# Streaming encoder layer on one core: weight-block sums fetched two units ahead, with other PSUM banks and another order of products

## The chip, the core and the metric

One core of a Trainium2 chip runs the whole program. The time is device microseconds from launch to the last output. The kernel before takes 1981.8 us (median of 3 runs, 1981.6 to 1982.52).

## What is computed

One inference step of a hybrid layer on 576 frames (512 of a prompt, 64 of a sample), model width 1024:

```python
h = h + 0.5 * swiglu(rmsnorm(h, g1), w_ffn1_in, w_ffn1_out)
h = h + mixer(rmsnorm(h, gm))
h = h + 0.5 * swiglu(rmsnorm(h, g2), w_ffn2_in, w_ffn2_out)
y = rmsnorm(h, final_norm)
def swiglu(x, w_in, w_out):
    a, b = split(x @ w_in, 2)            # w_in 1024 x 8192, w_out 4096 x 1024
    return (silu(a) * b) @ w_out
```

The mixer is one wide projection that feeds an SSD scan, a band attention and an mLSTM; their outputs are projected, gated, merged and projected once more. All is float32.

## The kernel before

**Products.** A float32 operand is split (`split`, L271) into a rounded part and a remainder: ScalarE (ACT) casts to `ph` (L272), VectorE (DVE) subtracts to `pl` (L273). A product of a 512 x 128 weight block with a 512 x 288 half of the activations is then 4 x 3 = 12 matmuls of 288 columns (`product`, L584, matmuls on L591). Most of the two feed-forward stages and of the mixer's projection is done in *units*: a 2 x 2 block product with seven products in place of eight. The weights of a unit are four blocks q0 to q3 in HBM; the operands on the weights' side are q0, q2, q3 (products A11, A22, A21) and the sums X1 = q0+q1, X2 = q1+q2, X3 = X1+q2, X4 = X3+q3. In each feed-forward stage a stream has 40 units, in the mixer 35.

**Fetching.** `fetch` (L436) loads q0,q1 into a tile `x12` of the ring `wx` (three buffers of 512 KB) from the SP queue (L444), then adds q1,q2 onto it with a second, accumulating transfer from GpSimd's (POOL's) queue (L445): that makes X1 and X2. POOL's queue waits in its turn until the load has landed. Three more loads from SP (L449) bring q0, q2, q3 into the ring `wr`. `operand` (L452) makes X3 and X4 by POOL additions (L455): in the feed-forward stages in place in `x12`, in the mixer in a ring `wy`.

**Order.** `stream` (L470) writes out the list of uses: round n holds the products of unit n marked 0 and those of unit n-1 marked 1 in `order`. In the feed-forward stages (L747) a round is X1, A22 of n-1, A11, A21 of n-1, X3, X4, X2 of n-1. Splits are written down AHEAD = 5 products before use (`make`, L477); `make` fetches unit n+1 when unit n's first operand, X1, is made. The third `wx` buffer is that of unit n-2, free when the X2 split of that unit is done, which is the split just before. Within these dependences and the priorities a planner (the framework's timeline scheduling) lays down the order in which each engine and queue gets its instructions; PE's order in the trace is not quite the written one. Every engine and queue works in order.

**Banks.** X1, X3, A22 and X2 of a unit add up in one PSUM bank, X4 and A21 in a second, A11 has a third (L749): two sets of three banks, alternating. Each partial sum is read out before the next product may add to it: `swiglu` (L594) copies X1 to `g` (ACT, L602) and X3 and X4 to `P` (ACT, L607), `residual` (L622) adds to `R` on DVE (L630). So product X3 waits for the copy L602, and X1 of unit n+2 for the last readout (L618 or L630) of unit n.

**Mixer.** `pairs` (L497) uses `stream` too, with its own order and banks, and the same `fetch`.

**Squares.** `sumsq` (L276) and the norms use tiles `sq` (two) and `na` (one) of 128 x 320 in the pool `small`.

Of the kernel before, what the change touches and what calls it, by code (L numbers as in the profile page):

```python
# [25 lines left out]
F32 = mybir.dt.float32  # L26
F32R = mybir.dt.float32r
AF = mybir.ActivationFunctionType
ALU = mybir.AluOpType
# [12 lines left out]
FBUFS = {"P": 5, "g": 5, "s": 3}  # L42
WBUFS = {"wr": 5, "wx": 3, "wy": 2, "ph": 6, "pl": 6}
PBUFS = {"s": 2, "x": 1, "v": 1}
# [34 lines left out]
class Hybrid:  # L79
    def __init__(self, ctx, tc, I, O):  # L80
        self.tc, self.nc, self.I, self.O = tc, tc.nc, I, O
        self.plan = []
        self.splan = []
# [57 lines left out]
    def hidden_tiles(self, name):  # L141

        self.hidden.close()
        self.hidden.enter_context(self.pools(name, yp=dict(side="right")))
        self.YH, self.YL = self.pair_of(self.yp, [128, 8, T], ("YH", "YL"))
# [34 lines left out]
    def ps(self, tag):  # L180
        return self.psp.tile([128, 512], F32, name="ps_" + tag, tag=tag, bufs=self.pbufs[tag])

    def sm(self):
# [92 lines left out]
    def sumsq(self, x, k, h, acc, first=None):  # L276
        nc = self.nc
        a, n = HALVES[h]
        if first is True or first is None and k == 0:
            nc.scalar.activation(acc[:, :n], x[:, k, a:a + n], AF.Square)  # L280
            return
        sq = self.small.tile([128, 320], F32, name="sq", tag="sq", bufs=2)
        nc.scalar.activation(sq[:, :n], x[:, k, a:a + n], AF.Square)
        nc.vector.tensor_tensor(acc[:, :n], acc[:, :n], sq[:, :n], op=ALU.add)
# [41 lines left out]
    def norm(self, x, g0, hi, lo):  # L326

        nc = self.nc
        with self.tc.high_priority(offset=1500):
            for h, (a, n) in enumerate(HALVES):  # L330
                sl = slice(a, a + n)
                acc = self.small.tile([128, 320], F32, name="na", tag="na", bufs=1)
                for k in range(8):
                    self.scaled(x, g0, hi, lo, k, sl)
                    self.sumsq(x, k, h, acc)
                pt = self.ps("x")
                self.total([acc], n, pt)
                nc.scalar.copy(self.rs[:, sl], self.spread(pt, n)[0][:, :n])

    def norm_first(self, x, g0, hi, lo, pin):  # L340
# [4 lines left out]
        for h, (a, n) in enumerate(HALVES):  # L345
            sl = slice(a, a + n)
            sq = self.sqp.tile([128, 8, n], F32, name="sq0", tag=f"sq{h}")
            pt = self.ps("x")
# [15 lines left out]
    def norm_out(self, x, g0, out):  # L364

        nc = self.nc
        with self.tc.high_priority(offset=1500):
            for h in (1, 0):
                a, n = HALVES[h]
                sl = slice(a, a + n)  # L370
                acc = self.small.tile([128, 320], F32, name="na", tag="na", bufs=1)
                pt = self.ps("x")
                for k in range(8):
                    if h == 0 and k == 7:
                        sq = self.small.tile([128, 320], F32, name="sq", tag="sq", bufs=2)
                        nc.scalar.activation(sq[:, :n], x[:, k, sl], AF.Square)
                        self.total([acc, sq], n, pt)
                    else:
                        self.sumsq(x, k, h, acc)
# [55 lines left out]

    def fetch(self, desc):  # L436

# [6 lines left out]
        nc.sync.dma_start(x12, src[:, 0:2, :])  # L444
        nc.gpsimd.dma_start(x12, src[:, 1:3, :], accum_op=ALU.add)  # L445
        raw = {"x12": x12}
        for q in (2, 3, 0) if self.mixer else (0, 2, 3):
            raw[q] = self.ring("wr")
            nc.sync.dma_start(raw[q], src[:, q, :])  # L449
        return raw  # L450

# [18 lines left out]
    def stream(self, seq, order, banks):  # L470
# [3 lines left out]
        uses = [(n - d, t) for n in range(len(seq) + 1) for d, t in order if 0 <= n - d < len(seq)]  # L474
        raw, ops, st = {}, {}, {}

        def make(n, t):  # L477
            for m in (n, n + 1):
                if m < len(seq) and m not in raw:
                    raw[m] = self.fetch(seq[m][0])  # L480
            ops[n, t] = self.operand(raw[n], t)
# [177 lines left out]
    def ffn(self, x, g0, win, wout, name, last=(0, 1)):  # L659
# [85 lines left out]
        for c in range(1, 4):  # L745
            seq += [unit(c, j) for j in range(2)] + [out(c - 1, m) for m in range(4)] + [unit(c, j) for j in range(2, 8)]
        order = ((0, self.T_X1), (1, self.T_A22), (0, self.T_A11), (1, self.T_A21), (0, self.T_X3), (0, self.T_X4),  # L747
                 (1, self.T_X2))
        self.stream(seq, order, lambda n: {t: 3 * (n % 2) + i for i, t in enumerate((self.T_X1, self.T_A11, self.T_X4))})  # L749
        self.drain()  # L750
# [608 lines left out]
    def run(self):  # L1359
        nc, tc = self.nc, self.tc  # L1360
        x = self.R1
        with self.ffn_phase("a"):
            xin = self.I["xT"].rearrange("(k p) t -> p k t", p=128)
            with self.pools("a0", sqp=None):
                self.setup()
# [34 lines left out]
    def branches(self, x):  # L1400
        nc = self.nc
        units = {"a": (self.attn_gemm, self.attn), "m": (self.ml_gemm, self.ml), "s": (self.ssd_gemm, self.ssd)}
        got = {u: units[u[0]][0](u[1]) for u in ORDER[:2]}
        with self.pools("m0", xp=None, op=None):
            self.XH, self.XL = self.pair_of(self.xp, [128, 8, T], ("XH", "XL"))
            self.norm(x, C_GM, self.XH, self.XL)
# [12 lines left out]
            self.plain([(("gate", 0), 1.0, put_gate)])  # L1419
        with self.pools("m", fp=None):  # L1420
            na = self.fp.tile([128, T], F32, name="sumsq")
            self.ss = [na[:, a:a + n] for a, n in HALVES]
# [113 lines left out]
```

## Time and profile before

| | |
|---|---|
| median of 3 runs | 1981.8 us |
| the profiled execution, its own time | 1983.52 us |
| its span, first to last instruction | 1981.8 us |
| PE (matmuls) busy | 1901.4 us, 96%, 13889 |
| DVE, ACT, POOL busy | 1461.5, 1083.3, 673.0 us |
| mean granted TensorE clock | 0.982 |
| mean DMA rate | 150 GB/s |
| chain that ended last | PE 35%, DMA 8%, DVE 3%, ACT 3%; by line L591 21%, the landing of `wx` 6% |
| first feed-forward stream (L591) | from 66 us |
| mixer | about 600 to 1215 us |
| second feed-forward stream (L591) | 1454 to 1913 us |

Busy shares are averages over these stages. A line such as "PE acc L591 <- ACT g L602: 4.2, 4, 1.8" says that matmuls of L591 began 4 times right after a wait that ACT's line 602 ended, 4.2 us in all, the longest 1.8 us. The ends of matmuls are modelled.

### The profile page before, as it was taken

The page shows a single profiled execution, that of the slowest core. Times are in us where ns is not written, and L with a number is a line of the kernel's source. Part 1 is how long each engine was busy: PE and PEld are TensorE (multiplying, and loading weights), DVE is VectorE, ACT ScalarE, POOL GpSimd, SP SyncE. Part 2 cuts the span into 40 slices and gives each one's busy share as a digit, 9 for nine tenths or more (in the row PEclk, how much of TensorE's full clock was granted, in tenths as well). Part 3 has the DMA queues.
Part 4 walks back from the last instruction along what each step waited for, and adds up shares of the span by engine and source line. Part 5 has one row for each costly group of instructions (what it writes and reads, how often), then busy time and mean ns, then how long its engine had stood idle before and what let it go on. Part 6 is the DMA issues. An engine that isn't in the chain of part 4 may idle for free.

```text
span 1981.8 us, 37575 instructions
## 1 busy us (share of the span) xinstructions
PE 1901.4 (96%) x13889; PEld 1824.5 (92%) x13889; DVE 1461.5 (74%) x2727; ACT 1083.3 (55%) x2487; POOL 673.0 (34%) x662
## 2 busy tenths in 40 slices
PE   9999999999999889999989998899999999999998
PEld 8899999999999759978889897899999999999998
DVE  8987877877668958667676774665798787787765
ACT  4554554544545577677586874333555454454444
POOL 5343333333202215322443443351233333333311
PEclk9999999999999879999999998999999999999999
DMA  7267666666742535753656668652236666656631
GB/s 215 72 158 174 151 155 163 149 167 168 184 128 96 131 104 145 212 149 110 178 150 180 162 169 246 203 167 86 75 97 160 160 150 161 162 151 161 174 109 63
DMA packets 130079, 297.04 MB, mean 150 GB/s; under 512 B 14416, under 2 KB 26320, under 8 KB 129896
## 3 DMA queue, kind: packets, MB, share of 16 engines
q1 hardware_dynamic: 100648, 208.03, 33.0%
q0 software_dynamic: 19760, 72.10, 19.9%
q10 hardware_dynamic: 9488, 14.52, 2.4%
q8 instruction: 109, 1.79, 0.4%
q14 instruction: 74, 0.61, 0.1%
HBM read 274.04 MB, written 20.56 MB: 149 GB/s over the span
## 4 chain that ended last, share of the span: by engine, by line
PE 35%; DMA 8%; DVE 3%; ACT 3%; issue 2%; POOL 1%; ACTq 0%; DVEq 0%; POOLq 0%; SPq 0%
PE acc L591 21%; PE acc L244 12%; DMA wx<-in_sblk 6%; DMA R<-scr_rows 1%; DVE pl L273 1%; ACT ph L272 1%; DMA y<-ys 1%; ACT R L1188 1%; DVE TL L273 0%; PE ps_s L1206 0%; PE ps_v L1228 0%; PE ps_x L1235 0%; DVE P L639 0%; DVE g L639 0%; DMA ys<-g 0%
## 5 line engine op out<-in xcount | busy, mean ns | idle before, releaser
L591 PE MATMUL acc<-TH,ph 128*128 128x288 f32 x3220 | 959.0, 300 | 31.9 <-ACT g L602 10.4
L591 PE MATMUL acc<-TL,ph 128*128 128x288 f32 x3220 | 952.8, 297 | 0.1
L591 PE MATMUL acc<-TH,pl 128*128 128x288 f32 x3220 | 944.1, 297 | 6.6 <-DVE pl L273 6.1
L591 PEld LDWEIGHTS acc<-TH,ph 128*128 128x128 f32 x3220 | 605.6, 189 | 52.3 <-ACT g L602 13.4
L591 PEld LDWEIGHTS acc<-TH,pl 128*128 128x128 f32 x3220 | 604.6, 189 | 14.3 <-DVE pl L273 11.1
L591 PEld LDWEIGHTS acc<-TL,ph 128*128 128x128 f32 x3220 | 607.8, 189 | 2.5 <-issue 1.9
L273 DVE TENSOR_TENSOR pl<-wr,ph 128x512 fp32r<-128x512 f32 x471 | 404.2, 863 | 83.4 <-ACT ph L272 76.3
L272 ACT CAST ph<-wx 128x512 fp32r<-128x512 f32 x390 | 233.4, 619 | 334.4 <-POOL wx L455 154.3
L273 DVE TENSOR_TENSOR pl<-wx,ph 128x512 fp32r<-128x512 f32 x390 | 286.1, 745 | 169.0 <-ACT ph L272 165.2
L272 ACT CAST ph<-wr 128x512 fp32r<-128x512 f32 x471 | 286.1, 616 | 202.9 <-PE acc L244 99.9
L455 POOL TENSOR_TENSOR wx<-wx,wr 128x512 f32<-128x512 f32 x160 | 226.0, 1413 | 446.0 <-DVE pl L273 411.8
L244 PE MATMUL acc<-YH,ph 128*128 128x256 f32 (+1 forms) x768 | 227.1, 300 | 9.0 <-DVE y L1303 5.3
L244 PE MATMUL acc<-YL,ph 128*128 128x320 f32 (+1 forms) x768 | 228.8, 299 | 2.1 <-DVE YL L323 2.1
L244 PE MATMUL acc<-YH,pl 128*128 128x320 f32 (+1 forms) x768 | 226.8, 298 | 0.0
L445 POOL DMA_DIRECT2D wx<-in_sblk x115 | 101.6, 892 | 239.1 <-DMA wx<-in_sblk 84.1
L244 PEld LDWEIGHTS acc<-YH,ph 128*128 128x128 f32 x768 | 146.9, 193 | 10.4 <-DVE y L1303 5.5
L244 PEld LDWEIGHTS acc<-YL,ph 128*128 128x128 f32 x768 | 146.8, 192 | 3.2 <-DVE YL L323 2.6
L244 PEld LDWEIGHTS acc<-YH,pl 128*128 128x128 f32 x768 | 146.5, 192 | 0.0
L455 POOL TENSOR_TENSOR wy<-wx,wr 128x512 f32<-128x512 f32 x35 | 51.4, 1468 | 184.2 <-DMA wx<-in_sblk 73.6
L630 DVE SCALAR_TENSOR_TENSOR R<-acc,R 128x288 f32<-128x288 f32 x168 | 73.2, 449 | 0.6 <-PE acc L591 0.4
L272 ACT CAST TH<-g 128x288 fp32r<-128x288 f32 x120 | 51.2, 433 | 38.6 <-DVE g L639 19.7
L616 POOL TENSOR_TENSOR g<-g,P 128x288 f32<-128x288 f32 x56 | 56.6, 1010 | 43.9 <-ACT P L615 43.9
(296 smaller groups left out, 2414.5 us busy)
## 6 DMA issues: line engine op xcount, KB each, us to landing
wr<-in_sblk SPq DMA_DIRECT2D x345, 256.0 KB, 4.3
wx<-in_sblk SPq DMA_DIRECT2D x115, 512.0 KB, 3.9
wx<-in_sblk POOLq DMA_DIRECT2D x115, 512.0 KB, 7.0
wr<-in_wblk SPq DMA_DIRECT2D x126, 256.0 KB, 3.2
R<-scr_rows ACTq DMA_DIRECT2D x12, 576.0 KB, 5.8
gs<-g SPq DMA_DIRECT2D x24, 288.0 KB, 4.7
y<-gs POOLq DMA_DIRECT2D x24, 288.0 KB, 3.4
y<-ys POOLq DMA_DIRECT2D x16, 288.0 KB, 4.4
```

The costliest lines, as they stand in the source:

```text
L244: nc.tensor.matmul(ps[:, :n], wt[:, wsl], xx[:, k0 + k, a:a + n], start=(k == 0 and i == 0), stop=(k == nk - 1 and i == 2))
L272: self.nc.scalar.copy(hi, src)
L273: self.nc.vector.tensor_tensor(lo, src, hi.bitcast(F32), op=ALU.subtract)
L445: nc.gpsimd.dma_start(x12, src[:, 1:3, :], accum_op=ALU.add)
L455: add = lambda o, one, two: self.nc.gpsimd.tensor_tensor(o, one, two, op=ALU.add)
L591: self.nc.tensor.matmul(ps, wt[:, wsl], xx[:, kk, :], start=(start and kk == 0 and i == 0), stop=(kk == 3 and i == 2), skip_group_check=True)
L616: nc.gpsimd.tensor_tensor(s["g"][:, 1, :], s["g"][:, 1, :], a, op=ALU.mult)
L630: self.nc.vector.scalar_tensor_tensor(o, ps, scale, o, op0=ALU.mult, op1=ALU.add)
L1188: nc.scalar.activation(e[:n, a:a + n], e[:n, a:a + n], AF.Relu, scale=-1.0, bias=self.TM[:n, c, tc_:tc_ + 1])
```

## The change

It does five things. `fetch` becomes `fetch_sums` (the load into `x12`, and a function that begins the adding transfer) and `fetch` (the three loads into `wr`). `make` now begins the load of unit n+2's sums when it makes X1 of unit n, and its adding transfer when it makes X3 of unit n, just ahead of that operand's POOL addition; the `wr` loads stay one unit ahead. `wx` gets a fourth buffer; its room comes from `sq` and `na`, which move from `small` to pools that exist in the stage anyway (`qp` in the feed-forward stages, buffers of `op` and `fp` in the mixer). In the feed-forward stages X2 of n-1 comes ahead of X4. There the banks become: X1 three in turn, A11 one, X4 two in turn. The mixer keeps its order and banks.

```diff
-WBUFS = {"wr": 5, "wx": 3, "wy": 2, "ph": 6, "pl": 6}
+WBUFS = {"wr": 5, "wx": 4, "wy": 2, "ph": 6, "pl": 6}
...
-        self.hidden.enter_context(self.pools(name, yp=dict(side="right")))
+        self.hidden.enter_context(self.pools(name, yp=dict(side="right"), qp=dict(side="right")))
+        self.sqp = self.qp, {"na": 1, "sq": 2}
...
+    def squares(self, tag):
+        pool, bufs = self.sqp
+        if pool is self.op:
+            return self.op.tile([128, T], F32, name=bufs[tag], tag=bufs[tag], bufs=2)[:, :320]
+        return pool.tile([128, 320], F32, name=tag, tag=tag, bufs=bufs[tag])
...
-        sq = self.small.tile([128, 320], F32, name="sq", tag="sq", bufs=2)
+        sq = self.squares("sq")
...
-    def fetch(self, desc):
+    def fetch_sums(self, desc):
...
         nc.sync.dma_start(x12, src[:, 0:2, :])
-        nc.gpsimd.dma_start(x12, src[:, 1:3, :], accum_op=ALU.add)
-        raw = {"x12": x12}
+        return {"x12": x12, "src": src}, lambda: nc.gpsimd.dma_start(x12, src[:, 1:3, :], accum_op=ALU.add)
+
+    def fetch(self, raw):
+
         for q in (2, 3, 0) if self.mixer else (0, 2, 3):
             raw[q] = self.ring("wr")
-            nc.sync.dma_start(raw[q], src[:, q, :])
-        return raw
+            self.nc.sync.dma_start(raw[q], raw["src"][:, q, :])
...
         def make(n, t):
-            for m in (n, n + 1):
-                if m < len(seq) and m not in raw:
-                    raw[m] = self.fetch(seq[m][0])
+
+            for m in range(n, min(n + 3, len(seq))):
+                if m not in raw:
+                    raw[m], begin[m] = self.fetch_sums(seq[m][0])
+                if m in begin and (m < n + 2 or t == self.T_X3):
+                    begin.pop(m)()
+                if m < n + 2 and 0 not in raw[m]:
+                    self.fetch(raw[m])
             ops[n, t] = self.operand(raw[n], t)
...
-        order = ((0, self.T_X1), (1, self.T_A22), (0, self.T_A11), (1, self.T_A21), (0, self.T_X3), (0, self.T_X4),
-                 (1, self.T_X2))
-        self.stream(seq, order, lambda n: {t: 3 * (n % 2) + i for i, t in enumerate((self.T_X1, self.T_A11, self.T_X4))})
+        order = ((0, self.T_X1), (1, self.T_A22), (0, self.T_A11), (1, self.T_A21), (0, self.T_X3), (1, self.T_X2),
+                 (0, self.T_X4))
+        self.stream(seq, order, lambda n: {self.T_X1: n % 3, self.T_A11: 3, self.T_X4: 4 + n % 2})
...
         with self.pools("m0", xp=None, op=None):
+            self.sqp = self.op, {"na": "xd", "sq": "xk"}
...
         with self.pools("m", fp=None):
+            self.sqp = self.fp, {"sq": 2}
```

## Rows read from the trace of the kernel before

**Rows 1.** Windows: each engine's busy us (x instructions), PEclk, DMA share, GB/s
```profile
66.30:100.00 33.70, 29.35 (x191) 26.94 (x190) 31.04 (x59) 19.45 (x47) 9.62 (x6) 0.95 0.33 91
100.00:531.00 431.00, 421.89 (x3139) 417.24 (x3138) 329.77 (x577) 222.83 (x469) 157.75 (x138) 1.00 0.65 161
1454.50:1912.90 458.40, 449.19 (x3328) 442.60 (x3327) 356.94 (x617) 236.93 (x506) 163.30 (x142) 1.00 0.60 154
640.00:1215.00 575.00, 544.11 (x3887) 487.04 (x3885) 414.23 (x848) 403.71 (x1071) 211.81 (x222) 0.97 0.58 156
```

**Rows 2.** Windows of L591 alone: PE busy, PEld busy, PEclk, DMA share, GB/s
```profile
1820.00:1900.00 80.00, 80.00 (x605) 80.00 (x604) 1.00 0.63 161
```

**Rows 3.** Waits of PE, 100 to 535 us: us in total, times, longest
```profile
PE acc L591 <- ACT g L602: 4.2, 4, 1.8
PE acc L591 <- DVE R L630: 3.0, 4, 1.0
PE acc L591 <- ACT P L607: 0.8, 4, 0.2
```

**Rows 4.** Waits of PE, 1454 to 1915 us
```profile
PE acc L591 <- ACT g L602: 6.2, 7, 2.0
PE acc L591 <- ACT P L607: 2.0, 7, 0.5
PE acc L591 <- DVE R L630: 0.4, 2, 0.3
```

**Rows 5.** Chain that ended last, in order of time: start us, us, what
```profile
1630.06 0.61 DVE pl L273
1630.69 3.95 DMA wx<-in_sblk
...
1634.92 8.63 DMA wx<-in_sblk
```

**Rows 6.** Timeline of ACT, 1640 to 1652 us: start, us, instruction, [idle before <-releaser]
```profile
1643.63 0.62 ACT L272 CAST ph<-wx 128x512 fp32r<-128x512 f32 x1 [3.73 <-DMA wx<-in_sblk]
...
1645.01 0.39 ACT L602 COPY g<-acc 128x288 f32<-128x288 f32 x1
```

**Rows 7.** Timeline of PE, 1644.5 to 1646.5 us
```profile
1645.45 0.40 PE L591 MATMUL acc<-TH,ph 128*128 128x288 f32 x1 [1.98 <-ACT g L602]
1645.69 0.29 PE L591 MATMUL acc<-TL,ph 128*128 128x288 f32 x1
```

**Rows 8.** Waits of ACT, 66 to 535 us
```profile
ACT ph L272 <- POOL wx L455: 74.7, 38, 3.9
ACT ph L272 <- DMA wx<-in_sblk: 50.0, 27, 3.7
```

**Rows 9.** Waits of ACT, 1454 to 1915 us
```profile
ACT ph L272 <- POOL wx L455: 78.3, 39, 3.8
ACT ph L272 <- DMA wx<-in_sblk: 55.4, 29, 3.7
```

**Rows 10.** DMA issues, whole span: KB each, median us to landing
```profile
wx<-in_sblk SPq DMA_DIRECT2D x115, 512.0 KB, 3.9
wx<-in_sblk POOLq DMA_DIRECT2D x115, 512.0 KB, 7.0
```

**Rows 11.** Waits of POOL, whole span
```profile
POOL wx L445 <- DMA wx<-in_sblk: 84.1, 54, 7.6
POOL wy L455 <- DMA wx<-in_sblk: 73.6, 14, 8.2
```

**Rows 12.** Timeline of POOL, 1640 to 1652 us
```profile
1645.05 1.28 POOL L455 TENSOR_TENSOR wx<-wx,wr 128x512 f32<-128x512 f32 x1 [6.33 <-DVE pl L273]
...
1648.91 0.87 POOL L445 DMA_DIRECT2D wx<-in_sblk  x1
```

**Rows 13.** Timeline of DVE, 1645 to 1646.5 us
```profile
1645.13 1.75 DVE L273 TENSOR_TENSOR pl<-wr,ph 128x512 fp32r<-128x512 f32 x1 [0.16 <-ACT ph L272]
```

**Rows 14.** Waits of ACT, 640 to 1210 us
```profile
ACT ph L272 <- DMA wx<-in_sblk: 5.7, 2, 4.5
```

More of the change, by code (lines that the diff above doesn't have):

```diff
@@ L81, in __init__ @@
         self.tc, self.nc, self.I, self.O = tc, tc.nc, I, O
+        self.op = None
         self.plan = []
@@ L331, in norm @@
                 sl = slice(a, a + n)
-                acc = self.small.tile([128, 320], F32, name="na", tag="na", bufs=1)
+                acc = self.squares("na")
                 for k in range(8):
@@ L346, in norm_first @@
             sl = slice(a, a + n)
-            sq = self.sqp.tile([128, 8, n], F32, name="sq0", tag=f"sq{h}")
+            sq = self.s0.tile([128, 8, n], F32, name="sq0", tag=f"sq{h}")
             pt = self.ps("x")
@@ L370, in norm_out @@
                 sl = slice(a, a + n)
-                acc = self.small.tile([128, 320], F32, name="na", tag="na", bufs=1)
+                acc = self.squares("na")
                 pt = self.ps("x")
@@ L374, in norm_out @@
                     if h == 0 and k == 7:
-                        sq = self.small.tile([128, 320], F32, name="sq", tag="sq", bufs=2)
+                        sq = self.squares("sq")
                         nc.scalar.activation(sq[:, :n], x[:, k, sl], AF.Square)
@@ L474, in stream @@
         uses = [(n - d, t) for n in range(len(seq) + 1) for d, t in order if 0 <= n - d < len(seq)]
-        raw, ops, st = {}, {}, {}
+        raw, ops, st, begin = {}, {}, {}, {}
         def make(n, t):
-            for m in (n, n + 1):
-                if m < len(seq) and m not in raw:
-                    raw[m] = self.fetch(seq[m][0])
+            for m in range(n, min(n + 3, len(seq))):
[5 more added lines that the diff above has]
+                    self.fetch(raw[m])
             ops[n, t] = self.operand(raw[n], t)
@@ L1363, in run @@
             xin = self.I["xT"].rearrange("(k p) t -> p k t", p=128)
-            with self.pools("a0", sqp=None):
+            with self.pools("a0", s0=None):
                 self.setup()
```

## The prediction

> **What bounds the kernel now.** I read the windows by stage first. In every stage PE is the engine that is nearly always busy, and TensorE's granted clock is 1.00 in both feed-forward streams (that is the 2.4 GHz level), so the time can only come from PE's idle stretches. PE stands idle for 431.00 - 421.89 = 9.1 us in the steady part of the first stream, 458.40 - 449.19 = 9.2 us in the second stream, 33.70 - 29.35 = 4.4 us where the first one starts, and 575.00 - 544.11 = 30.9 us in the mixer [rows 1].
>
> Idle time understates the loss, because the ends of matmuls are modelled. So I take the pace instead: in a stretch of the second stream without a pause PE starts 605 matmuls in 80.00 us, 0.1322 us each [rows 2]. By that pace 3139 matmuls need 415.0 us and the window of 431.0 loses 16.0 us; 3328 need 440.0 and the window of 458.4 loses 18.4 us [rows 1]. Together **34.4 us** are lost in the steady streams, 1.88 times the 18.3 us of idle time. One pause shows why: idle for 1.98 us, and the matmul after it is followed by the next one at 0.24 us where the pace is 0.13 [rows 2, 7].
>
> Next, who ends PE's pauses. In the two streams it is the copy of X1 (L602) with 4.2 + 6.2 = 10.4 us, the readouts L630 with 3.0 + 0.4 = 3.4, and the copies L607 with 0.8 + 2.0 = 2.8, together 16.6 of the 18.3 [rows 3, 4]. These are small instructions. They are late because their engine, which works in order, stands at something else. ACT's timeline shows at what: at 1643.63 the cast of X1's weights begins after 3.73 us of waiting for the landing in `wx`; the copy L602 stands behind it and starts at 1645.01; PE goes on at 1645.45 [rows 6, 7]. The chain gives the landing's own history: the third buffer comes free at 1630.67 with a split, the load takes 3.95 us, the adding transfer, begun at 1634.92, takes 8.63 [rows 5]. Over the two streams ACT waits for this landing 27 + 29 times, 50.0 + 55.4 us, and for POOL's sums 38 + 39 times, 74.7 + 78.3 us [rows 8, 9]. Most of it is swallowed by the five products that operands are made ahead (5 x 12 x 0.1322 = 7.9 us); what is not is PE's loss.
>
> **The adding transfer moved.** Count in products of 12 x 0.1322 = 1.59 us. Before, the buffer for unit n+1 comes free with X2 of n-2 (last of round n-1), and X1 of n+1 is due 8 products later, 12.7 us. Load and adding transfer need 3.95 + 0.3 + 8.63 = 12.9 us in the chain [rows 5], 3.9 + 7.0 in the median [rows 10]: just in time at best, hence the waits. After, the load for n+2 begins when X2 of n-2 (now one place earlier) frees a buffer, the adding transfer stands at X3 of n, 6 products or 9.5 us later, and X1 of n+2 comes 10 products or 15.9 us after that. Even 8.63 us leave 7 us. So ACT's waits for the landing should go. What is late next is POOL's sums, on which ACT already waits.
>
> The Trainium skill ("DMA: Bandwidth & Descriptors", section "Anatomy of one DMA — SWDGE (gpsimd) path") has a fit for a transfer from this queue by which 512 KB take an estimated 3.2 us. By it X1 would never be late and this term of the sum would be nil. The traced transfer of 8.63 us and the median of 7.0 [rows 5, 10] disagree, and the measurement decides.
>
> What the move is worth: the L602 share of the loss is 10.4 x 1.88 = 19.6 us. I take nine tenths, 17.6. Of the L607 share (2.8 x 1.88 = 5.3) I take half, 2.6, since those copies stand behind POOL's sums as well. Of the remaining 1.7 us of idle time I take nothing.
>
> **Banks.** X2 of unit n is written one round after X1 of n, and X1 of n+2 starts the next round in the same bank, so it waits for the last readout: L630, 3.4 x 1.88 = 6.4 us. With three banks in turn that readout has a whole round more. I take all 6.4; the lower end is 3, because ACT's waiting delays these readouts too and the landing alone may account for half. A11's single bank is read 7 products before its next use, and costs nothing.
>
> **Order.** X4's sum overwrites X3's in place, so it needs X3's split first. With X2's cast between, ACT has 0.62 us [rows 6] of other work while POOL adds. Against that, A21 now adds onto X4's bank three products after X4 in place of four, 4.8 us for a copy of 0.4 us, and X2 follows A22's readout by three in place of four. I take nothing either way; bounds: +2 and -2 us.
>
> **Queues passed.** On POOL the issue of the adding transfer, 0.87 us [rows 12], now stands directly ahead of X3's sum. Before, POOL stood at it until the load had landed, 54 times, 84.1 us in all [rows 11]; with 9.5 us from load to add it should rarely wait. If it does, X3's sum behind it waits too, then ACT. On SP the load of n+2 stands where that of n+1 stood, ahead of the same three `wr` loads, waiting for a split of the same unit. The number of transfers, sums, casts and matmuls is the same. The tiles `sq` and `na` serve the norms at the stages' borders, and where they share buffers with the operands of the next step they are done first: nothing, and if that cover is gone a few casts of half a microsecond, +-1 us.
>
> **Mixer.** It gets the earlier transfers, not the banks. ACT waits for the landing there only twice, 5.7 us [rows 14]; POOL's sums for the mixer wait 14 times, 73.6 us [rows 11]. PE's 30.9 us of idle time there is mostly the scans' and attention's. Not shown is how much of it hangs on these 14 sums. From above, one such long wait per two units at a loss like L602's, some 6 us; from below, a planner that lays the mixer out anew may also lose 4. I take a gain of 2, nearer to zero because ACT's row is small. The first stream's start (33.70 us, of which 25.3 by the pace) is DVE's, busy 31.04 of it [rows 1]: nothing.
>
> **Sum.** 17.6 + 2.6 + 6.4 + 2 = 28.6, less 2 for short new waits where POOL's sums are now last: a gain of 26.6 us. From the profiled execution's own 1983.5 us this gives 1956.9; the median of the runs is 1.7 us below that execution, so I say **1955 us**. Its own range is 1948 to 1963. What a measurement of this kernel can tell from no change is about 0.2%, 4 us.
>
> **Rival A: the sums take the landing's place.** ACT waits longer for POOL's sums than for the landing (153.0 against 105.4 us, [rows 8, 9]). If those waits lengthen when the others go, the shares of L602 and L607 fall only by 105.4 / 258.4 = 0.41: 0.41 x 24.9 + 3 for the banks = 13, so 1969 us (1964 to 1975). For it: a POOL sum of 1.28 us beside a split on DVE makes that split 1.75 us, against 0.61 for the one in the chain [rows 5, 12, 13], and each unit has two such sums. Against it: in the pauses that I followed the landing is last, and the sum only begins after it [rows 6, 12]. The Trainium skill ("SBUF — State Buffer", section "Who interferes with whom") says that a VectorE instruction with two SBUF inputs and a GpSimd instruction that reads SBUF exclude each other for a whole instruction; the stretched split agrees, and by that rule both sums of a unit go on costing DVE about 1 us each. Chance 0.20.
>
> **Rival B: more than the streams.** All 34.4 us go, and the mixer gives 6: some 1941 us. For it: the margins above. Against: DVE is busy 76 to 78% of the streams [rows 1], so not every pause can go. Chance 0.08.
>
> **Rival C, slower: POOL stands at the adding transfer, ahead of X3's sum.** It decides where the load lands more than 9.5 us after its buffer came free, that is when SP is held 5.6 us or more by the `wr` loads ahead of it (9.5 - 3.9). Today's 56 landing waits cost 24.9 us (L602 and L607), 0.44 each; at 80 stream units, 36 us are paid for the 26.6 won: 1991 us. Against it: the buffer and SP's place stay as they are, and POOL's waits average 1.6 us [rows 11]. Chance 0.07.
>
> **Rival D: it does not do what it says.** The planner lays down the order on each queue, and may put load and adding transfer where they stood. Then only part of the banks remains, 3 us: 1979. Chance 0.07.
>
> **Numbers.** Forecast 0.58, A 0.20, B 0.08, C 0.07, D 0.07. The range 1941 to 1975 holds the forecast, A and B and leaves out C and D. Faster by over 0.2%: 0.58 + 0.20 + 0.08 = 0.86, of which A's upper edge gives 0.01 away: 0.85. Within: 0.08. Slower: 0.07.
>
> **What would show it.** ACT's wait for the landing of `wx` in the streams gone or under 10 us; POOL's wait for the load at L445's successor near zero; the pauses by L602 and L630 mostly gone; the second stream near 445 us for its 458. Still 7 us per adding transfer. A shows itself by ACT's waits for POOL's sums above 153 us with PE pausing for L602 as before; C by POOL waiting for the load at the adding transfer; D by loads and adding transfers as close together as now. The prediction is wrong if the landing waits go and PE's idle time in the streams stays above 9 us.

## The result, and the profile after

The changed kernel takes **1960.6 us** (median of 4 runs, 1956.5 to 1963.6), the kernel before, run beside it, 1981.7 us (1980.0 to 1982.5). The ratio is 0.9892, 95% interval 0.9874 to 0.9911: 21.1 us or 1.1% faster, against 26.6 us in the prediction's sum. The profiled execution is the fastest of the four, 1956.5 us with a span of 1954.7, where the one of before had 1981.8.

Where did the 27.1 us between the two spans come from? I measure each stream from its first to its last matmul and take what lies around them. First before, then after, in windows of the stream's line alone (columns: length, PE busy, PEld busy, PEclk, DMA share, GB/s).

```profile
66.28:530.98 464.70, 451.23 (x3324) 443.93 (x3324) 1.00 0.62 156
1454.50:1912.91 458.41, 449.20 (x3324) 442.37 (x3324) 1.00 0.60 154
```

The same view of the changed kernel, whose stream line is L606:

```profile
66.65:520.05 453.40, 446.57 (x3324) 442.31 (x3324) 1.00 0.63 160
1438.18:1886.33 448.15, 445.74 (x3324) 442.25 (x3324) 1.00 0.60 156
```

The streams give 464.70 - 453.40 = 11.3 and 458.41 - 448.15 = 10.3 us, together 21.6. The stretch between them goes from 1454.50 - 530.98 = 923.5 to 1438.18 - 520.05 = 918.1, 5.4 less; start and end give the last 0.1. By the prediction's pace of 0.1322 us 3324 matmuls take 439.4 us, so the loss against that pace fell from 44.2 us to 22.7 for the two streams, the start included. Half of it is still there.

By stage, all engines (columns as in [rows 1]):

```profile
100.00:531.00 431.00, 428.88 (x3210) 426.57 (x3210) 383.67 (x587) 230.77 (x474) 159.23 (x140) 1.00 0.66 167
640.00:1215.00 575.00, 544.34 (x3897) 487.95 (x3895) 410.11 (x854) 402.53 (x1070) 217.98 (x230) 0.97 0.61 165
```

PE's idle time in the first of these windows fell from 9.1 us to 2.1; in the mixer it is 30.7, as before [rows 1]. One column grew by more than its instructions: DVE is busy 383.67 us for 587 of them, where 577 took 329.77.

The pauses of PE that [rows 3, 4] showed, after, from 100 to 535 us and from 1440 to 1900 us (us in total, times, longest):

```profile
PE acc L606 <- ACT g L617: 1.1, 3, 0.7
PE acc L606 <- DVE P L625: 0.8, 3, 0.3
...
PE acc L606 <- DVE P L625: 1.3, 5, 0.3
PE acc L606 <- ACT P L622: 0.6, 3, 0.2
PE acc L606 <- ACT g L617: 0.2, 1, 0.2
```

The copy of X1 (L602, now L617) fell from 10.4 us to 1.3, the readouts L630 are gone, the copies L607 (now L622) went from 2.8 to 0.6. What ACT's casts wait for, 66 to 525 us and 1438 to 1890 us:

```profile
ACT ph L281 <- PE acc L606: 65.0, 85, 1.0
ACT ph L281 <- POOL wx L465: 61.9, 45, 3.5
...
ACT ph L281 <- PE acc L606: 77.8, 99, 1.0
ACT ph L281 <- POOL wx L465: 43.4, 35, 2.9
```

The landing of `wx` is in neither list: 105.4 us of waiting [rows 8, 9] are 0. The waits for POOL's sums did not take their place; they fell from 153.0 us to 105.3. What ACT waits for most now is PE reading its operands; in those waits it is ahead of PE.

POOL's wait for the load at the adding transfer, after, whole span, answers to [rows 11]:

```profile
POOL wx L454 <- DMA wx<-in_sblk: 102.4, 21, 8.2
```

Fewer waits (21 for 54), but 102.4 us for 84.1; inside the two streams 37.6 us in 10 waits, 43.4 in 46 before. That line undercounts. In the streams of the changed kernel POOL is idle for 355 us just before these issues, and most of it stands under DVE's name. Of the 55 issues there whose load has its landing on record, 53 came after an idle stretch and within 0.6 us of that landing, so POOL stood there for the load. Before, it was 38 of 56, and POOL was idle 119 us.

Next the groups that grew, in the list of the costliest groups, before (busy us, mean ns; idle time and its releaser):

```profile
L273 DVE TENSOR_TENSOR pl<-wr,ph 128x512 fp32r<-128x512 f32 x471 | 404.2, 863 | 83.4 <-ACT ph L272 76.3
...
L273 DVE TENSOR_TENSOR pl<-wx,ph 128x512 fp32r<-128x512 f32 x390 | 286.1, 745 | 169.0 <-ACT ph L272 165.2
...
L455 POOL TENSOR_TENSOR wx<-wx,wr 128x512 f32<-128x512 f32 x160 | 226.0, 1413 | 446.0 <-DVE pl L273 411.8
```

The same groups after:

```profile
L282 DVE TENSOR_TENSOR pl<-wr,ph 128x512 fp32r<-128x512 f32 x471 | 450.7, 962 | 89.3 <-ACT ph L281 78.6
...
L282 DVE TENSOR_TENSOR pl<-wx,ph 128x512 fp32r<-128x512 f32 x390 | 322.3, 831 | 31.1 <-ACT ph L281 24.2
...
L465 POOL TENSOR_TENSOR wx<-wx,wr 128x512 f32<-128x512 f32 x160 | 245.6, 1535 | 194.8 <-DVE pl L282 156.7
```

The same 861 splits on DVE cost 46.5 + 36.2 = 82.7 us more, and POOL's sums 19.6 us more. The timelines of POOL and of DVE show one case (start us, us):

```profile
1635.93 0.88 POOL L454 DMA_DIRECT2D wx<-in_sblk  x1 [5.44 <-DVE TL L282]
1636.54 1.60 POOL L465 TENSOR_TENSOR wx<-wx,wr 128x512 f32<-128x512 f32 x1
...
1636.22 2.48 DVE L282 TENSOR_TENSOR pl<-wr,ph 128x512 fp32r<-128x512 f32 x1
1638.63 0.44 DVE L629 TENSOR_TENSOR P<-acc,P 128x288 f32<-128x288 f32 x1
1638.99 0.68 DVE L282 TENSOR_TENSOR pl<-wr,ph 128x512 fp32r<-128x512 f32 x1
```

A split that takes 0.68 us undisturbed takes 2.48 when POOL's issue of an adding transfer and a sum stand back to back beside it. (The 0.61 us that the prediction set beside 1.75 is a piece of the chain and not a whole split.) The issue itself came after 5.44 us of idle time, 0.54 us after the load's landing at 1635.40. In the streams of the changed kernel the issue is followed at once by a sum 70 times in 74, before 11 times in 73. I call a split's time beyond 0.68 us *held*, where the split is over 0.8 us, and add it up over 100 to 520 and 1440 to 1885 us: 69 us before, 147 after. Over each kernel's own streams it is up to 4.3 us more.

### The profile page after: what moved, and what is told of

It is laid out like the page before. It is cut to its first block, busy times and chain, and to the rows that moved or that the text cites. A ratio compares the mean times of both kernels' runs of the same rounds, so it can differ in the third digit from the quotient of the medians.

```text
span 1954.7 us, 37719 instructions
## 1 busy us (share of the span) xinstructions
PE 1891.3 (97%) x13889; PEld 1822.7 (93%) x13889; DVE 1550.4 (79%) x2727; ACT 1095.9 (56%) x2487; POOL 674.5 (35%) x662
## 5 line engine op out<-in xcount | busy, mean ns | idle before, releaser
L606 PE MATMUL acc<-TH,ph 128*128 128x288 f32 x3220 | 960.3, 299 | 17.8 <-ACT uv L524 7.1
L606 PE MATMUL acc<-TL,ph 128*128 128x288 f32 x3220 | 954.8, 297 | 1.1 <-DVE TL L282 1.1
L606 PE MATMUL acc<-TH,pl 128*128 128x288 f32 x3220 | 951.4, 297 | 3.9 <-DVE pl L282 3.9
L606 PEld LDWEIGHTS acc<-TH,ph 128*128 128x128 f32 x3220 | 606.4, 189 | 35.1 <-ACT uv L524 9.8
L606 PEld LDWEIGHTS acc<-TH,pl 128*128 128x128 f32 x3220 | 607.5, 189 | 8.8 <-DVE pl L282 4.8
L606 PEld LDWEIGHTS acc<-TL,ph 128*128 128x128 f32 x3220 | 607.8, 189 | 2.5 <-DVE TL L282 1.7
L282 DVE TENSOR_TENSOR pl<-wr,ph 128x512 fp32r<-128x512 f32 x471 | 450.7, 962 | 89.3 <-ACT ph L281 78.6
L282 DVE TENSOR_TENSOR pl<-wx,ph 128x512 fp32r<-128x512 f32 x390 | 322.3, 831 | 31.1 <-ACT ph L281 24.2
L465 POOL TENSOR_TENSOR wx<-wx,wr 128x512 f32<-128x512 f32 x160 | 245.6, 1535 | 194.8 <-DVE pl L282 156.7
L253 PE MATMUL acc<-YH,pl 128*128 128x256 f32 (+1 forms) x768 | 227.9, 298 | 0.0
L253 PEld LDWEIGHTS acc<-YH,ph 128*128 128x128 f32 x768 | 146.9, 193 | 10.3 <-DVE y L1318 5.6
L281 ACT CAST TH<-g 128x288 fp32r<-128x288 f32 x120 | 51.5, 432 | 61.4 <-POOL g L631 34.4
L465 POOL TENSOR_TENSOR wy<-wy,wr 128x512 f32<-128x512 f32 x35 | 47.9, 1370 | 76.7 <-DVE pl L282 48.3
```

The source lines that it names most:

```text
L253: nc.tensor.matmul(ps[:, :n], wt[:, wsl], xx[:, k0 + k, a:a + n], start=(k == 0 and i == 0), stop=(k == nk - 1 and i == 2))
L281: self.nc.scalar.copy(hi, src)
L282: self.nc.vector.tensor_tensor(lo, src, hi.bitcast(F32), op=ALU.subtract)
L465: add = lambda o, one, two: self.nc.gpsimd.tensor_tensor(o, one, two, op=ALU.add)
L606: self.nc.tensor.matmul(ps, wt[:, wsl], xx[:, kk, :], start=(start and kk == 0 and i == 0), stop=(kk == 3 and i == 2), skip_group_check=True)
```

## The experiments

The **theory** that I took from the prediction: the fetch removes ACT's landing waits, the banks remove other pauses, and the two gains add. Against it stand that fetch and banks remove the same pauses, so that either alone gives most of the gain; that the written place of the adding transfer decides; and, from the profile after, that the new place of its issue on POOL gives time back, through DVE's held splits or through sums that start late behind it. All streams below are measured as above; "streams" is their sum, "held" as just defined, both from the one profiled execution of each kernel. Each ratio is to the runs of the kernel before that were made beside that kernel (medians 1981.7 to 1983.1 us).

| kernel | median us | ratio to before, 95% | streams us | held us |
|---|---|---|---|---|
| before | 1981.7 | 1 | 923.1 | 69 |
| changed | 1960.6 | 0.9892 [0.9874, 0.9911] | 901.6 | 147 |
| e8, changed, again | 1958.8 | 0.9881 [0.9856, 0.9905] | 898.6 | 139 |
| e1, new fetch alone | 1955.0 | 0.9857 [0.9827, 0.9887] | 893.9 | 64 |
| e7, new banks alone | 1962.4 | 0.9896 [0.9872, 0.9921] | 904.4 | 99 |
| e3, changed, old order | 1963.0 | 0.9903 [0.9873, 0.9932] | 901.2 | 84 |
| e12, changed, old banks | 1966.1 | 0.9926 [0.9912, 0.9941] | 902.3 | 142 |
| e9, changed, adding at A11 | 1962.0 | 0.9899 [0.9876, 0.9922] | 901.8 | 146 |
| e4, changed, adding at once | 1962.3 | 0.9895 [0.9869, 0.9922] | 899.8 | 157 |
| e10, e1, adding at A11 | 1955.2 | 0.9866 [0.9841, 0.9891] | 893.9 | 60 |
| e5, e1, adding a unit later | 1957.8 | 0.9886 [0.9857, 0.9914] | 893.2 | 62 |
| e14, 4th buffer alone | 1955.5 | 0.9875 [0.9856, 0.9894] | 893.9 | 61 |
| e13, before, copy on DVE | 1978.8 | 0.9981 [0.9964, 0.9997] | 924.8 | 65 |
| e11, issue behind the sum | 1943.8 | 0.9813 [0.9796, 0.9831] | 891.6 | 81 |

### The parts alone

**e1**, the changed kernel with the old order and the old banks:

```diff
-        order = (..., (0, self.T_X3), (1, self.T_X2), (0, self.T_X4))
-        self.stream(seq, order, lambda n: {self.T_X1: n % 3, self.T_A11: 3, self.T_X4: 4 + n % 2})
+        order = (..., (0, self.T_X3), (0, self.T_X4), (1, self.T_X2))
+        self.stream(seq, order, lambda n: {t: 3 * (n % 2) + i for i, t in enumerate((self.T_X1, self.T_A11, self.T_X4))})
```

> The change with the old banks and the old order of products in the feed-forward stages: only the fetch two units ahead and the adding transfer moved. My theory (the landing of the adding transfer held ACT, and ACT held PE): 1965 to 1970 us, 12 to 17 us below the kernel before; ACT's wait for the landing in the two streams falls from 105 us to under 10; PE goes on pausing for the last readout before X1 (4 us of idle time). Rival (the banks gave most, the lead of five products hid the landing): 1975 us or more, and the streams' lengths stay within 5 us of before.

**e7**, the kernel before with the new banks alone (three buffers for `wx`, old fetch, old order; the norms' tiles lie as in the changed kernel):

```diff
-        self.stream(seq, order, lambda n: {t: 3 * (n % 2) + i for i, t in enumerate((self.T_X1, self.T_A11, self.T_X4))})
+        self.stream(seq, order, lambda n: {self.T_X1: n % 3, self.T_A11: 3, self.T_X4: 4 + n % 2})
```

> The kernel before with the new banks alone (X1 three in turn); fetch, three buffers and order of products as before. My theory: 1974 to 1979 us, the pauses before X1 gone, ACT still waiting for the landing some 100 us in the streams. Rival (the banks gave most): 1966 us or less.

Windows of the stream line, e1 and then e7:

```profile
66.19:516.58 450.39, 445.86 (x3324) 443.21 (x3324) 1.00 0.64 161
1444.71:1888.25 443.54, 442.19 (x3324) 441.47 (x3324) 1.00 0.62 157
```

```profile
65.70:516.99 451.29, 445.56 (x3324) 442.23 (x3324) 1.00 0.63 161
1438.68:1891.76 453.08, 446.11 (x3324) 442.34 (x3324) 1.00 0.62 156
```

The fetch alone takes 923.1 - 893.9 = 29.2 us out of the streams, the banks alone 18.7, the whole change 21.6 (24.5 in e8). Both kernels came out below what was expected of them, and e7 where its rival had put it. Two gains that would add to 48 give 22 to 25 together: they remove the same loss, and the whole is worse than the better half.

How banks can do this without touching a transfer, ACT's timeline of e7 shows:

```profile
1575.24 0.62 ACT L281 CAST ph<-wx 128x512 fp32r<-128x512 f32 x1
1575.77 0.39 ACT L615 COPY g<-acc 128x288 f32<-128x288 f32 x1
1577.15 0.62 ACT L281 CAST ph<-wx 128x512 fp32r<-128x512 f32 x1 [1.00 <-DMA wx<-in_sblk]
```

ACT still waits for the landing in e7 (35.5 + 42.8 us in the streams, 50 times, for 105.4 and 56; the two lines stand below, 66 to 525 and 1438 to 1890 us), but here the copy of X1 (L615) stands ahead of the waiting cast; before, it stood two or three instructions behind it [rows 6].

```profile
ACT ph L281 <- DMA wx<-in_sblk: 35.5, 24, 3.4
...
ACT ph L281 <- DMA wx<-in_sblk: 42.8, 26, 3.6
```

In the second stream of the kernel before, 21 of the 23 full `swiglu` rounds are read out as A22, X1, A11, A21 or A22, X1, A21, A11, for X1, A22, A11, A21 as written. In e7 all 23 full rounds have the written order: X1 is first and its copy is due earlier. So the wait is still there, and less that PE needs stands behind it.

### The changed kernel's two small edits, on top of the fetch

**e3**, the changed kernel with the old order (new banks stay):

```diff
-        order = (..., (0, self.T_X3), (1, self.T_X2), (0, self.T_X4))
+        order = (..., (0, self.T_X3), (0, self.T_X4), (1, self.T_X2))
```

> The change with the old order of products (X3, X4, X2) but the new fetch and banks. My theory: the order costs and gives little, within 3 us of the changed kernel; the short pauses for the readout of A22 (L625 of the changed kernel, 0.27 us each) go, since X2 comes four products after A22 again. Rival (the order carries the gain, since X4's sum stands right behind X3's): 8 us or more slower than the changed kernel, with PE pausing for the copies of X1 and X3.

**e12**, the changed kernel with the old banks (new order stays):

```diff
-        self.stream(seq, order, lambda n: {self.T_X1: n % 3, self.T_A11: 3, self.T_X4: 4 + n % 2})
+        self.stream(seq, order, lambda n: {t: 3 * (n % 2) + i for i, t in enumerate((self.T_X1, self.T_A11, self.T_X4))})
```

> The changed kernel with the banks of before: new fetch, new order of products, two banks for X1. It tells apart banks and order, which between them lengthen the streams from 894 us (new fetch alone) to 899 to 902. If the order costs it: 899 or more, splits held over 120 us. If the banks cost it: 893 to 896, and the run 1953 to 1957. A third way, that X1 stands right behind X2 and X4 in the same bank: pauses of PE before X1, streams over 905.

**e8** is the changed kernel without an edit, for the spread between two profiled executions.

> The changed kernel once more, for its spread: its four runs lie between 1956.5 and 1963.6 us, twice as wide as those of the kernel before. If the spread comes from TensorE's granted clock, the runs with a mean clock of 0.985 are near 1957 and those with 0.981 near 1963, and a profile of a long run differs from that of a short one in stretches of the mixer; if it comes from contention of transfers, the clock is the same in both.

With e1 these make a square. Streams: old banks and old order 893.9, new banks 901.2, new order 902.3, both 898.6 to 901.6. On top of the new fetch each edit alone costs 7 to 8 us, and the second costs nothing more. The medians say the same: 8 us for e3 over e1, 11 for e12, 4 to 6 for both edits. The held time goes with the order: 142 us in e12 and 147 in the changed kernel, 84 and 64 with the old order. In e3 the issue is mostly followed by the readout's multiplication on POOL (50 times in 74), in e12 by the sum (71 times). How that reaches PE, e12 shows: its waits of PE from 66 to 525 us, and one of them:

```profile
PE acc L606 <- DVE pl L282: 7.1, 10, 1.4
...
412.93 0.40 PE L606 MATMUL acc<-TH,pl 128*128 128x288 f32 x1 [0.99 <-DVE pl L282]
```

Ten of PE's pauses in the two streams from 100 us on end with a split; eight of these splits were held, for 1.5 to 2.7 us in place of 0.68, and end 6.6 us of idle time. So there the order's cost is seen at its place. But it all falls into e12's first stream (458.1 us for e1's 450.4). The second has more held time (79 us, 66 in the first) and is only 0.6 us longer than e1's: a held split costs where PE is about to need it. The banks' cost is not placed: e3 has only 20 us more held time than e1, and its pauses sit at the copies L622 (2.6 + 2.4 us), which in e1 come to 0.5 + 0.6. Why those are late with three banks I can't say from these runs. e8, the spread, has runs of 1959.1, 1956.7, 1961.1 and 1958.6 us at mean clocks of 0.981, 0.984, 0.983 and 0.984; the clock orders them only loosely.

### Does the written place of the adding transfer matter?

**e4** (adding transfer right behind its load), **e9** (at A11, one turn earlier), both on the changed kernel; **e10** (at A11) and **e5** (only when it is due for the next unit), both on e1. All four edit one condition:

```diff
-                if m in begin and (m < n + 2 or t == self.T_X3):
+                if m in begin:
+                if m in begin and (m < n + 2 or t == self.T_A11):
+                if m in begin and m < n + 2:
```

The first new line is that of e4, the second that of e9 and e10, the third that of e5.

> The changed kernel with the adding transfer begun right behind its load, not four products later; still two units ahead. My theory: POOL stands at it until the load has landed, some 3.8 us per unit less what it idles anyway, and X3's sum behind it has 4 products of room: POOL's waits for the load rise well above 102 us, PE loses little, within 4 us of the changed kernel. Rival (rival C of the prediction: POOL standing at the load makes the sums late): 10 us or more slower than the changed kernel.

> The changed kernel, but the adding transfer is begun at A11 of unit n, two products behind the load and two ahead of X3, so that its issue on POOL is not back to back with X3's sum. My theory now (the new fetch and the new banks remove the same stall; what the two together lose against the new fetch alone is DVE, whose splits are held while POOL issues and adds in one go): DVE's splits in the two streams are held some 70 to 90 us beyond their usual length in place of 139 to 147, the streams together take 893 to 897 us for the 899 to 902 of the changed kernel, and the run 1953 to 1956 us. Rival (the banks or the order themselves cost it, as A11 has one bank and A21 and X2 come one product sooner): streams 899 us or more, time as the changed kernel, 1957 to 1961.

> The new fetch alone (old banks, old order), with the adding transfer begun at A11 in place of X3. My theory: the splits on DVE are hardly held in the new fetch alone (64 us), so nothing is to be won: 1953 to 1958 us, streams 893 to 896 us. Rival (POOL stands at the adding transfer, which now comes two products sooner after its load): POOL's waits for the load grow and the streams lengthen by 5 us or more.

> The new fetch with old banks and old order, but the adding transfer begun only when X1 of the unit before is made, 7 products ahead of its use: the load comes two units ahead, the adding transfer as late as before, with no load to wait for. It parts the load's landing from the adding transfer's. 7 products are 11.1 us and the transfer takes 6 to 8.6: my theory is that most of the landing waits go all the same, 0 to 20 us of them left for 105, and 1953 to 1962 us. Rival (it is the adding transfer's own early start that matters): 50 us or more of landing waits stay and the time is 1968 or more.

The compiled programs of e4 and e9 have the changed kernel's order of instructions on every engine, those of e10 and e5 that of e1: the planner lays the issue so early in POOL's queue that it goes out some 4.2 us behind the load's issue in all of them (and in the kernel before), 0.3 to 0.5 us after its landing. So the written distance does nothing here, and what was expected of e9, a gain by parting issue and sum, and of e4 and e5 was not put to the test. The times are those of repeats and give the spread: one order has streams of 898.6 to 901.8 us (medians 1958.8 to 1962.3), the other 893.2 to 893.9 (1955.0 to 1957.8). The two bands don't touch.

**e14** goes further: the fetch of before, written one unit ahead with the adding transfer right behind, and only the fourth buffer, with the squares' tiles moved for its room:

```diff
-WBUFS = {"wr": 5, "wx": 3, "wy": 2, "ph": 6, "pl": 6}
+WBUFS = {"wr": 5, "wx": 4, "wy": 2, "ph": 6, "pl": 6}
```

> The kernel before with a fourth buffer in the ring of the sums (and the squares' tiles moved, which makes its room): the fetch is written one unit ahead as before, with banks and order of before. If what is written decides: the load still begins one unit ahead, landing waits of 80 us or more, 1975 to 1983. If the ring decides, because the planner begins a load as soon as a buffer is free: landing waits under 20 us and 1953 to 1960, as the new fetch alone.

```profile
65.47:515.73 450.26, 445.88 (x3324) 443.24 (x3324) 1.00 0.64 161
1438.87:1882.51 443.64, 442.18 (x3324) 441.46 (x3324) 1.00 0.62 157
```

893.9 us, as e1, and no landing wait. Its compiled program has e1's order on every engine. So the fourth buffer is the whole of the fetch's gain; the written distance of two units adds nothing to it.

### Taking the copy away from the waiting engine

**e13**, the kernel before, with X1's copy on DVE, which does not wait for the landing:

```diff
-                nc.scalar.copy(s["g"][:, 1, :], ps)
+                nc.vector.tensor_copy(s["g"][:, 1, :], ps)
```

> The kernel before with one edit: the copy of X1 (L602) goes from ACT to DVE; fetch, banks and order as before, so ACT waits for the landing as before. My theory (PE pauses since that copy stands two or three places behind ACT's wait for the landing): the landing waits stay near 100 us, but the pauses at L602 (10.4 us of idle time) go, and the run gains 10 to 20 us: 1963 to 1973. Rival (the landing itself, through X1's operands, holds PE): the pauses stay under another name, 1977 us or more.

PE's waits in e13, 100 to 535 us (us in total, times, longest):

```profile
PE acc L591 <- DVE g L618: 1.8, 4, 0.7
PE acc L591 <- DVE R L630: 1.2, 3, 0.8
PE acc L591 <- DVE g L602: 1.2, 3, 0.5
```

The pause at L602 is nearly gone (10.4 us before, 1.2 in both streams), ACT still waits 80.4 us for the landing, and the streams are no shorter: 924.8 for 923.1. The ratio, 0.9981 [0.9964, 0.9997], is a gain of 0.2%, 0.4% at the most, where 10 to 20 us were expected. The next to come late took over: L618 with 4.4 us and L630 with 3.5 in the two streams. The planner laid out ACT's and DVE's order anew around the moved copy, so this is not that one instruction alone. Even so, PE's loss did not go with the instruction that ended the pause. When the landing's wait goes (e14), 29 of the 44 us over the pace go; I read the loss as work on DVE and ACT that bunches behind the landing.

### The issue taken out from ahead of the sum

**e11**, the changed kernel, with the issue of the adding transfer held behind X3's sum by an order constraint in the streams; in the mixer it is only written there (`last_sum` is X3's sum on POOL):

```diff
-                if m in begin and (m < n + 2 or t == self.T_X3):
+                if m in begin and m < n + 2:
...
+            if t == self.T_X3 and n + 2 in begin:
+                with (nullcontext() if self.mixer else self.tc.issue_after(self.last_sum.ins)):
+                    begin.pop(n + 2)()
```

> The changed kernel with the issue of the adding transfer queued behind X3's sum on POOL in the feed-forward stages (an order that the planner has to keep; where it is merely written, the planner moved it back). My theory (issue and sum in one go hold DVE's splits): splits held 60 to 95 us in place of 139 to 157, the two streams 893 to 897 us in place of 899 to 902, the run 2 to 6 us below the changed kernel. Rival (banks or order of products cost it): splits held less, streams still 899 or more.

Windows of e11's stream line (L610), columns as before:

```profile
65.43:514.97 449.54, 445.89 (x3324) 443.47 (x3324) 1.00 0.64 163
1431.36:1873.46 442.10, 442.09 (x3324) 441.86 (x3324) 1.00 0.62 159
```

DVE's two groups of splits in e11:

```profile
L282 DVE TENSOR_TENSOR pl<-wr,ph 128x512 fp32r<-128x512 f32 x471 | 390.8, 834 | 98.5 <-ACT ph L281 83.2
...
L282 DVE TENSOR_TENSOR pl<-wx,ph 128x512 fp32r<-128x512 f32 x390 | 319.3, 822 | 37.1 <-ACT ph L281 22.6
```

And ACT's waits for POOL's sums in e11, 66 to 525 us and 1431 to 1880 us:

```profile
ACT ph L281 <- POOL wx L466: 19.5, 17, 2.9
...
ACT ph L281 <- POOL wx L466: 8.4, 11, 1.1
```

A split beside sum and issue in that order, from the timelines of POOL and of DVE in e11:

```profile
1542.88 1.29 POOL L466 TENSOR_TENSOR wx<-wx,wr 128x512 f32<-128x512 f32 x1 [3.26 <-DVE pl L282]
1544.12 0.87 POOL L454 DMA_DIRECT2D wx<-in_sblk  x1
...
1543.70 1.02 DVE L282 TENSOR_TENSOR pl<-wr,ph 128x512 fp32r<-128x512 f32 x1
```

**1943.8 us**, the best of all: 16.8 below the changed kernel's median, with no overlap of their runs (1943.2 to 1944.7), where 2 to 6 were expected. In the second stream PE has no idle time left (442.10 - 442.09), ACT waits 27.9 us for POOL's sums where the changed kernel had 105.3, and the held time falls from 147 us to 81. The streams are 9.9 us shorter; the span 12.8. Issue and sum stand back to back in that order only twice in 74.

Two things changed at once here. Splits are held less, and sums start earlier: 69 of the changed kernel's sums right behind an issue start 2.33 us (mean) after the split that they need, the others 0.08 us (median), and in e11 the same 69 start 0.08 us after it (median). In the changed kernel POOL stood at the issue until the load had landed, and the sum stood behind it. Which of the two gave the 9.9 us, no run here parts. For the splits speak e12's pauses; against late sums as the whole account, e1 has 126.0 us of ACT's waits for sums, more than the changed kernel, and shorter streams.

What else stays open: e11 has the new banks, and e3, also with the new banks and nearly its held time (84 us), but with the old order, is 9.5 us slower in the streams, so held time is not the whole account. The old banks under e11's rule were not run. And against e1 the streams of e11 are only 2.3 us shorter. Most of the 11.2 us between their medians lies in the stretch between the streams, 916.4 us in e11's profile and 928.1 in e1's, and no run here explains it.

## Why the prediction was right, and where its sum was not

The direction, the bound and the landing wait as the main stall held: 1960.6 against 1955, in the forecast's own range of 1948 to 1963. The sign it gave for being wrong, idle time of PE above 9 us with the landing waits gone, did not appear: 2.1 + 2.4 us in the windows where [rows 1] had 9.1 + 9.2. Point by point:

- **The loss by the pace, 34.4 us.** Right in kind. Idle time goes on understating it: the changed kernel's second stream has 2.4 us idle and is 8.7 us over the pace's 439.4.
- **The adding transfer moved, 17.6 + 2.6.** The mechanism is shown (no landing wait in the changed kernel, e1 or e14). Its size was too low: alone it gives 29.2 us in the streams, with both starts. The failing step is the pricing of a pause by the instruction that ends it ("the L602 share"): in e13 that share went away and the time did not, in e1 more went away than bore that name.
- **Its cause.** I priced the written places: the load a unit earlier and the adding transfer 9.5 us behind it. The planner begins the adding transfer some 4.2 us behind the load in every kernel, and e14 shows that the buffer alone decides. The cause as written is wrong, its effect right.
- **Banks, 6.4.** Wrong as an addition. Alone they give 18.7 us (e7), on top of the fetch they cost 7 (e3 against e1). The step that failed is the sum itself: it split one loss among edits each of which can remove most of it.
- **Order, 0, bounds +2 and -2.** Missed: 902.3 against 893.9 in the streams of e12 and e1, a loss of 8 us. The prediction saw that the issue "now stands directly ahead of X3's sum" and took it that POOL "should rarely wait" there. POOL stood there for the load in nearly every unit, and the prediction did not ask what the two in a row do to DVE, though it had the row of a split held by one sum [rows 13].
- **Less 2 for short new waits.** Mis-sized, and at the same place: e11, which takes the issue from ahead of the sum, has 9.9 us back in the streams. ACT's waits for the sums, which is what the prediction had in mind, did not grow in total (105.3 us for 153.0), but in e11, with the sum first, they are 27.9.
- **Mixer, +2.** Not shown. The stretch between the streams was 923.5 us before, 918.1 in the changed kernel's profile and 924.7 in e8's. Those two are one program. They differ in granted clock: from 700 to 740 us, inside the mixer, it is 0.87 and 0.79, a mean over stretches at the 2.4 and at the 1.2 GHz level. First the changed kernel, then e8 (columns as in [rows 1]):

```profile
700.00:740.00 40.00, 35.94 (x215) 24.45 (x215) 23.33 (x63) 29.09 (x89) 7.72 (x10) 0.87 0.29 84
```

```profile
700.00:740.00 40.00, 34.76 (x189) 22.98 (x189) 21.28 (x60) 25.96 (x81) 6.18 (x10) 0.79 0.24 65
```

  A gain of 2 us can't be told from this. It also bears on the median: the profiled execution has a mean clock of 0.985 and 1956.5 us, the other three 0.981 to 0.983 and 1958.5 to 1963.6.
- **Rival A** fell: its sign was ACT's wait for POOL's sums above 153 us, and it is 105.3.
- **Rival C** came true in its mechanism and not in its price. I wrote that POOL's wait for the load would be near zero. In the streams POOL stood at 53 of 55 issues until the load had landed, and 69 sums behind them started 2.33 us late in the mean. It came about otherwise than C says: loads did not take longer (3.8 us to landing in the median, 3.9 before), but the planner began the adding transfer some 4.2 us behind the load in place of 9.5. C's price, 36 us, did not fall due; what part of e11's 9.9 us belongs to the late sums is open. Waiting for the load alone does not cost it: in e1 POOL waits 92.9 us there in the streams, 61 times, but mostly not directly ahead of a sum, and e1 has shorter streams than the changed kernel.
- **Rival D** was half right: the planner does put the adding transfer where it stood. The buffer, which D left out, brought the gain all the same.
- **B's time** was reached, by another kernel: e11's 1943.8 is 2.8 us above it.

Two errors cancel: the fetch was undervalued by 9.0 us in the streams (29.2 for 20.2), and banks, order and short waits, entered as 6.4 + 0 - 2 = +4.4, cost 4.7 to 7.6 there (29.2 less the 24.5 and 21.6 of the whole change). That the sum came within 5.5 us of the 21.1 measured is, in that part, luck.

## What to carry to other kernels

When two edits aim at the same stall, price each alone and the pair as the larger of the two, and then ask what the smaller one costs when the stall is already gone; here the better half beat the whole. Price a stall by the wait that bunches the work and not by the instruction that happens to end PE's pause: here taking that instruction away moved the pause to others. Before a DMA issue that waits for a load is put ahead of work on the same queue, ask what that work will wait for. And where a planner orders the queues, compare the orders of the two compiled programs first; what is written at another place may be the same program, while one more buffer, or an order that is enforced, is a different one.

## What was not expected of the hardware

What a POOL instruction costs a DVE instruction with two SBUF inputs depends on how long POOL's work still runs when the split begins. In the windows used above all 14 traces together have 1597 held splits, and every one of them ends 0.55 to 0.56 us after the end of a sum or a multiplication on POOL that it overlapped: 2.48 us in the case above, where the sum ends at 1638.14 and the split at 1638.70, and 1.02 us in the case of e11. So a split that begins late beside a sum is held little, and one caught by a sum with the readout's multiplication right behind it is held through both. In the changed kernel those held beside one sum alone are held 0.82 us (mean of 54), beside an issue and then a sum 1.73 (20), beside sum and multiplication 1.73 (17), beside all three 2.34 (15). In e11, where the issue comes behind the sum, a held split beside the two is held 0.54 us (43), no longer than beside a sum alone there (0.57, 74). Beside an issue alone none is held (17 splits in the changed kernel).

What an issue directly ahead of a sum changes is who is caught. In the changed kernel 27 splits that began up to 0.48 us ahead of such a sum were held to its end or beyond, while 22 that began 0.43 to 0.69 us ahead got through; ahead of sums without an issue, eight splits that began 0.15 to 0.21 us earlier all got through.

The Trainium skill ("SBUF — State Buffer", section "Who interferes with whom") says that such an instruction and a GpSimd instruction that reads SBUF lock each other out for a whole instruction. The fixed 0.55 us from POOL's end to the split's end agrees. A split held by a sum that begins after it, behind a GpSimd DMA issue, goes beyond that sentence; no run here shows what in the issue keeps DVE out. And 66 us less held time (147 to 81) came with 9.9 us less in the streams, while e12's second stream has 79 us of it and is 0.6 us longer than e1's: DVE's stretched instructions cost only where PE was about to need them.
